# Three of eight experts computed with two products per weight block, a sixth of their blocks unsplit

## The chip, the cores and the metric

The kernel is one program on one core of one Trainium2 chip. The metric is the device time of one execution in microseconds, the median of three runs.

## The reference, cut to what matters

A small network of two blocks runs on 256 tokens of width 1024 in float32. Its last layer, to which the change belongs, is a mixture of eight experts, each a gated feed-forward net of width 3584. A router picks two experts for each token. The reference computes all experts for all tokens and weighs them with the gates, which are zero for experts that a token did not choose:

```
gates = sum of softmax(top 2 logits) * one_hot(top 2 experts, 8)
for e in range(8):
    h_e = silu(t @ w1[e]) * (t @ w3[e])          # 256x1024 @ 1024x3584
    out = out + gates[:, e:e+1] * (h_e @ w2[e])  # 3584x1024
```

## The kernel before

The weights are float32 in the chip's memory and the work runs block by block on them. `Weights` lists all weight keys in order of use; SyncE (SP) loads one 1 MB key at a time into a ring of raw buffers (`load`, L342), and waits for a buffer whose old content has been split. In the expert stage the ring has 15 buffers. Each key is two blocks of 128x1024. `make` splits a block into two float32r halves: ScalarE (ACT) rounds it to `whi` (L371), VectorE (DVE) subtracts to get `wlo` (L372). There are four buffers for each half, and `get` lets `make` run three blocks ahead of the block in use.

[...] Three products stand for one float32 product: high by high, high by low, low by high. A unit is the work on one block; in the expert stage it holds 2 x 3 = 6 products of 512 columns.

The tokens of an expert are gathered into 128 slots (`CAP`). `moe_choose` takes the logits, marks the two largest (`msel`), and counts places with two small products (`mpos`). `moe_slots` makes one-hot matrices `pe`. `moe_gather`, run for two experts at once, multiplies the token halves by `pe` and copies high and low parts of the gathered tokens to `gx`. `moe_units` then orders an expert's units: for each of seven blocks of 512 hidden columns, 4 units of `e1`, 4 units of `e3`, then 4 units of `e2` of the block before. After the last `e1` unit of a block ACT takes a tanh of the sum and DVE multiplies (L2340, L2341); after the last `e3` unit DVE multiplies again (L2345). `turn` transposes the result and splits it into `room` (L429, L430). At the end `moe_scatter` multiplies by the transposed one-hot matrix `ptm` and adds to `acc` (L2504). An expert has 42 keys, so 84 units. The order on PE, ACT and DVE is the order in which the program is written (`manual_schedule`): each engine takes its instructions in that order.

If an expert has more than 128 tokens, a branch at the end (`tc.If(most > over)`) runs the whole stage a second time.

Of the kernel before, what the change touches and what calls it, by code (L numbers as in the profile page):

```python
# [22 lines left out]
P = 128  # L23
# [10 lines left out]
DEEP = 8, 3, 1  # L34
HALVES = slice(0, 64), slice(64, 128)
# [161 lines left out]
def _consts():  # L197
# [34 lines left out]
    c["tie"] = np.zeros((P, 64)) + (np.arange(8)[None, :] < np.arange(8)[:, None]).astype(float).reshape(1, 64)  # L232
    t = np.arange(S)
# [22 lines left out]
LATE = ("flip", "cos", "sin", "rd", "sel", "oh", "ohm", "tri", "ones", "iota", "tie")  # L256
# [51 lines left out]
class Weights:  # L308


    def __init__(self, nc, w, ring, parts, tails, keys, ahead):
        self.nc, self.w, self.ring, self.parts, self.tails = nc, w, ring, parts, tails
        self.subs = []
        off, _ = _offsets()
        for key in keys:
            for i in range(len(off[key][1])):
                self.subs.append((key, i))
        self.ahead = ahead
        self.made, self.used = 0, 0
        self.ready = []  # L320
        self.keys, self.sent, self.loaded = keys, 0, deque()

# [6 lines left out]
    def load(self, between=None):  # L329

        nc = self.nc
        off, subs = _offsets()[0][self.keys[self.sent]]
# [4 lines left out]
        src = self.w[off : off + P * sum(subs)].rearrange("(p n w) -> p n w", p=P, n=n)  # L337
# [12 lines left out]

    def make(self):
# [9 lines left out]
        res = []  # L361
        for tail in range(1 + (subs[i] > 1024)):
# [23 lines left out]
class Net:  # L386
# [1928 lines left out]
    def moe_units(self, st, e, gather, scatter, first, last):  # L2315

        nc = self.nc
        loc = {"h": []}
        p = st["p"]

        def up(nm, nb, kh, i):
            def g(hi, lo):
                if kh == 0 and i == 0:
                    loc[nm] = self.bank("mm")
                xh, xl = st["xh", e], st["xl", e]
                for kk in range(2):
                    k = kh * 4 + i * 2 + kk
                    wh, wl = hi[:, kk * 512 : kk * 512 + 512], lo[:, kk * 512 : kk * 512 + 512]
                    self.mm(loc[nm], xh[:, k, :], wh, k == 0, False)
                    self.mm(loc[nm], xh[:, k, :], wl, False, False)  # L2330
                    self.mm(loc[nm], xl[:, k, :], wh, False, k == 7)
                if kh == 1 and i == 1:
                    act(nm, nb)

            return g

        def act(nm, nb):
            if nm == "e1":
                t = self.keep.tile([P, 512], F32, name="mt", tag="sq_acc")
                nc.scalar.activation(t, loc["e1"], AF.Tanh, scale=st["rs", e][:, 0:1])  # L2340
                nc.vector.scalar_tensor_tensor(t, t, 1.0, loc["e1"], op0=ALU.add, op1=ALU.mult)  # L2341
                loc["t"] = t
            else:
                t = loc["t"]
                nc.vector.scalar_tensor_tensor(t, t, st["rs", e][:, 1:2], loc["e3"], op0=ALU.mult, op1=ALU.mult)  # L2345
                loc["done"] = t

        def turn(a=0, z=4):
            t = loc["done"]
            ps = self.bank()  # L2350
            for i in range(a, z):
                self.transpose(ps[:, i * P : i * P + P], t[:, i * P : i * P + P])
            hh, hl = st["act"]
# [3 lines left out]
        def down(j, i):  # L2357
            def g(hi, lo):
# [62 lines left out]
    def moe_gather(self, st, e):  # L2421
# [7 lines left out]
        def part(c2):  # L2429
            def f():  # L2430
                if c2 == 0:
                    loc["t"] = [self.keep.tile([P, 8, 2, P], F32R, name="gx", tag=tag) for tag in ("xgh", "xgl")]
                    for a in range(2):
                        st["xh", e + a], st["xl", e + a] = [t[:, :, a, :] for t in loc["t"]]
                pe, t = loc["pe"], loc["t"]
                for part, src in enumerate((st["hh"], st["hl"])):
# [6 lines left out]
                    o = t[part][:, 2 * c2 : 2 * c2 + 2].rearrange("p c a s -> p (c a s)")  # L2443
                    if part and e == 0:
                        nc.vector.tensor_copy(o, ps)
                    else:
                        nc.scalar.activation(o, ps, AF.Copy)
# [62 lines left out]
    def moe_slots(self, st, e, n=2):  # L2510

        pe = st["q"].tile([P, 2, 2, P], F32R, name="pe", tag="pe")
        for a in range(n):
            for th in range(2):
                pos, sel = st["pos"][:, th, e + a : e + a + 1], st["sel"][:, th, e + a : e + a + 1]
                self.nc.vector.tensor_scalar(pe[:, th, a, :], st["iota"], pos, sel, op0=ALU.is_equal, op1=ALU.mult)
# [41 lines left out]
    def moe_load(self, st):  # L2558
# [3 lines left out]
        for k in ("tri", "ones", "iota", "tie"):  # L2562
# [38 lines left out]
    def moe_choose(self, st):  # L2601
# [28 lines left out]
        st["sel"] = sel.bitcast(F32).rearrange("p (a e) -> p a e", a=2)  # L2630
# [16 lines left out]
        num = q.tile([P, 8], F32, name="num")  # L2647
        self.copy(num, cnt[:, 0:8])
        st["num"] = num
        st["sq"] = self.squares(self.x, 3, nc.gpsimd)  # L2650

    def moe_prelude(self, st, p):
# [11 lines left out]
        def gates():  # L2664
            st["most"] = q.tile([P, 1], F32, name="most")
            nc.vector.tensor_reduce(st["most"], st["num"], axis=AX.X, op=ALU.max)
            lg, sel = st["lg"], st["sel"]
            mx = q.tile([P, 2], F32, name="lmx")
# [11 lines left out]
        return [scales, gates]  # L2680
# [35 lines left out]
def _program(tc, io, out, tap=None, stop=None, over=CAP):  # L2716
    nc = tc.nc
    with ExitStack() as ctx:
# [27 lines left out]
        with tc.tile_pool(name="moe", bufs=1) as p:  # L2746
            deeper = net.ws.deepen(net.open_pool, DEEP[2])[0]
            st["row"] = (deeper, io["rows"][1:2, :].partition_broadcast(P))
            net.moe_all(st, net.run, net.moe_prelude(st, p), out)
# [3 lines left out]
            most = nc.values_load(flag[0:1, 0:1], min_val=0, max_val=S)  # L2753
            with tc.If(most > over):
                nc.vector.tensor_scalar(st["pos"], st["pos"], -float(CAP), None, op0=ALU.add)
                for f in net.moe_gather(st, 0):
                    f()
                net.ws = Weights(nc, io["w"], deque([net.raw] * 3), net.parts, None, _moe_keys(), 3)
                net.moe_all(st, net.run, [], None)
# [15 lines left out]
```

## Time and profile before

| | us |
|---|---|
| median of 3 runs | 2690.24 (2688.87 to 2690.79) |
| the profiled execution | 2689.64 |
| its span, first to last instruction | 2687.8 |
| PE busy in the span | 2635.4 (98%) |
| DVE busy | 2060.2 (77%) |
| ACT busy | 1607.8 (60%) |

The expert stage is the last thousand microseconds of the span: the first product with gathered tokens (`gx`) starts at 1666.7 us and the last with hidden units (`room`) at 2672.2 us. PE is busy nearly all of the time, and the profile counts pipelined products that overlap only once, so a busy PE says how long its queue was never empty.

### The profile page before, as it was taken

How to read it: one execution, taken by the hardware profiler on the slowest of the kernel's cores; microseconds unless marked ns; L12 is line 12 of the kernel's file. 1: busy time of each engine (PE TensorE's matmuls, PEld its weight loads, DVE VectorE, ACT ScalarE, POOL GpSimd, SP SyncE). 2: the span in 40 equal slices, each digit the busy share in tenths (PEclk: the TensorE clock that was granted, in tenths of full speed). 3: DMA queues.
4: the chain of work that ended last, by engine and by line, in shares of the span. 5: the costliest groups of instructions: out<-in, count | busy, mean ns of one | idle time of the engine just before them, and what ended most of it. 6: DMA issues, size and time to landing. Idle time of an engine off the chain costs nothing.

```text
span 2687.8 us, 44169 instructions
## 1 busy us (share of the span) xinstructions
PE 2635.4 (98%) x17854; PEld 2401.2 (89%) x17854; DVE 2060.2 (77%) x2581; ACT 1607.8 (60%) x2153; POOL 131.3 (5%) x130
## 2 busy tenths in 40 slices
PE   8999999999999999999999999999999999999998
PEld 7989999999989999999999999878887888787876
DVE  5875767556784766557866677999999999999997
ACT  4433555445533555445644456777777777777776
POOL 0032000000012100000000000000000000000000
PEclk9999999999999999999999999999999999999999
DMA  6423534545432543544385445999899989998991
GB/s 245 144 87 108 203 142 165 188 180 202 146 99 92 188 158 126 187 177 157 127 312 187 172 155 206 367 352 366 327 360 354 359 330 358 360 358 330 359 358 59
DMA packets 100285, 614.80 MB, mean 229 GB/s; under 512 B 10664, under 2 KB 20392, under 8 KB 32232
## 3 DMA queue, kind: packets, MB, share of 16 engines
q1 hardware_dynamic: 99352, 609.78, 61.7%
q8 instruction: 142, 2.33, 0.4%
q0 software_dynamic: 720, 2.11, 0.2%
q14 instruction: 71, 0.58, 0.1%
HBM read 609.22 MB, written 2.11 MB: 227 GB/s over the span
## 4 chain that ended last, share of the span: by engine, by line
PE 90%; DVE 5%; issue 3%; ACT 1%; POOL 0%; DMA 0%; SPq 0%; ACTq 0%; DVEq 0%; POOLq 0%
PE ps_mm L422 59%; PE ps_b L422 29%; PE ps_b L426 2%; DVE wlo L372 2%; ACT whi L371 1%; DVE xgl L509 0%; ACT xgh L508 0%; DMA wraw<-in_w 0%; DVE room L430 0%; DVE mt L2341 0%; DVE acc L2504 0%; DVE xc L1894 0%; POOL st_tm_y L451 0%; POOL hn_v L451 0%; POOL tk L1174 0%
## 5 line engine op out<-in xcount | busy, mean ns | idle before, releaser
L372 DVE TENSOR_TENSOR wlo<-wraw,whi 128x1024 fp32r<-128x1024 f32 (+1 forms) x1129 | 1366.2, 1230 | 382.7 <-ACT whi L371 372.6
L371 ACT ACTIVATE whi<-wraw 128x1024 fp32r<-128x1024 f32 (+1 forms) x1129 | 1177.7, 1055 | 754.9 <-PE ps_mm L422 565.0
L422 PE MATMUL ps_mm<-xgh,whi 128*128 128x256 f32 x2048 | 589.0, 288 | 10.8 <-ACT whi L371 7.4
L422 PE MATMUL ps_mm<-whi,gx 128*128 128x512 f32 x1792 | 591.2, 400 | 0.0
L422 PE MATMUL ps_mm<-xgh,wlo 128*128 128x256 f32 x2048 | 582.2, 285 | 4.6 <-DVE wlo L372 4.6
L422 PE MATMUL ps_mm<-xgl,whi 128*128 128x256 f32 x2048 | 582.6, 285 | 0.0
L422 PEld LDWEIGHTS ps_mm<-whi,gx 128*128 128x128 f32 x1792 | 337.5, 188 | 79.3 <-issue 0.5
L422 PEld LDWEIGHTS ps_mm<-xgh,whi 128*128 128x128 f32 x2048 | 391.3, 191 | 15.6 <-ACT whi L371 7.4
L422 PEld LDWEIGHTS ps_mm<-xgh,wlo 128*128 128x128 f32 x2048 | 388.8, 190 | 6.3 <-DVE wlo L372 6.1
L422 PEld LDWEIGHTS ps_mm<-xgl,whi 128*128 128x128 f32 x2048 | 389.4, 190 | 2.3 <-issue 1.4
L422 PE MATMUL ps_mm<-wlo,gx 128*128 128x512 f32 x896 | 355.0, 396 | 0.2 <-DVE wlo L372 0.2
L422 PE MATMUL ps_b<-whi,room 128*128 128x512 f32 x896 | 294.6, 397 | 0.0
L422 PEld LDWEIGHTS ps_mm<-wlo,gx 128*128 128x128 f32 x896 | 168.8, 188 | 39.1 <-issue 0.7
L422 PEld LDWEIGHTS ps_b<-whi,room 128*128 128x128 f32 x896 | 168.3, 188 | 39.4 <-issue 0.2
L422 PE MATMUL ps_b<-hl,whi 128*128 128x256 f32 x688 | 194.5, 283 | 0.0
L422 PE MATMUL ps_b<-hh,wlo 128*128 128x256 f32 x688 | 194.4, 283 | 0.0
L422 PE MATMUL ps_b<-hh,whi 128*128 128x256 f32 x688 | 193.9, 283 | 0.0
L422 PE MATMUL ps_b<-wlo,room 128*128 128x512 f32 x448 | 176.8, 395 | 0.0
L422 PEld LDWEIGHTS ps_b<-hh,wlo 128*128 128x128 f32 x688 | 132.0, 192 | 0.0
L422 PEld LDWEIGHTS ps_b<-hl,whi 128*128 128x128 f32 x688 | 131.9, 192 | 0.0
L422 PEld LDWEIGHTS ps_b<-hh,whi 128*128 128x128 f32 x688 | 131.5, 192 | 0.2
L422 PEld LDWEIGHTS ps_b<-wlo,room 128*128 128x128 f32 x448 | 84.2, 188 | 19.4 <-issue 0.2
(545 smaller groups left out, 3562.6 us busy)
## 6 DMA issues: line engine op xcount, KB each, us to landing
wraw<-in_w SPq DMA_DIRECT2D x557, 1024.0 KB, 5.5
wrawt<-in_w SPq DMA_DIRECT2D x32, 256.0 KB, 4.7
wraw<-in_w SPq DMA_DIRECT2D x8, 512.0 KB, 3.3
cmpw<-in_cmpw SPq DMA_DIRECT2D x2, 1024.0 KB, 7.3
mem<-in_memt SPq DMA_DIRECT2D x2, 1024.0 KB, 7.9
wraw<-in_w SPq DMA_DIRECT2D x2, 560.0 KB, 5.9
x<-in_xt SPq DMA_DIRECT2D x4, 256.0 KB, 5.7
c_rd<-in_cst SPq DMA_DIRECT2D x2, 512.0 KB, 7.6
```

The source lines that it names most:

```text
L371: nc.scalar.activation(hi[:, c], src[:, c], AF.Copy)
L372: nc.vector.tensor_sub(lo[:, c], src[:, c], hi[:, c].bitcast(F32))
L422: self.nc.tensor.matmul(out, lhsT, rhs, start=start, stop=stop, **kw)
L426: self.nc.tensor.transpose(out, in_, self.ident[:k, :k])
```

## The change

The eight experts get places 0 to 7 that are not their numbers any more. Expert 0 keeps place 0. The other seven are ranked by the number of tokens that chose them; the three with the fewest take places 1, 3 and 5 and are called light, and have 64 slots (`LCAP`) instead of 128. The router's tables are reordered by place (`moe_places`, `placed`), and the loads of places 1 to 7 take their address from a register of SP, which is filled from the table `place` (`places`).

A light expert has the 64 slots twice: columns 0 to 63 of the stationary operand hold the high part of the tokens, columns 64 to 127 the low part. One product with `whi` and one with `wlo` then give all four partial products, in two halves of the rows. After each `e1` and `e3` sum, `fold` copies the lower half from PSUM with ACT, and one product by an identity adds it to the upper half; this product is put after the next unit's products (`late`). For `e2` the same doubling is used and the scatter adds the halves.

In a light expert every first block of the keys `e3` with `kh` 0 and of every second `e2` key is not split (`whole`): 14 of 84 blocks. There PE multiplies the raw float32 block in two full float32 products instead of four float32r ones.

If a light expert has more than 64 tokens or another more than 128, the branch at the end runs the second pass.

```diff
+LIGHT, LCAP = (1, 3, 5), 64
...
+    heavy = [p for p in range(N_EXP) if p not in LIGHT]
+    c["rank"] = np.zeros((P, 8)) + np.argsort(np.array(heavy + list(LIGHT)))[None, :]
+    c["lead"] = np.zeros((P, 8)) + 1e6 * (np.arange(8) == 0)[None, :]
...
+        self.place, self.light = {}, ()
+        self.stride = off["e1", 1, 0, 0][0] - off["e1", 0, 0, 0][0]
...
-        off, subs = _offsets()[0][self.keys[self.sent]]
+        key = self.keys[self.sent]
+        off, subs = _offsets()[0][key]
         self.sent += 1
         pool = self.ring.popleft()
         self.ring.append(pool)
         n, m = len(subs), min(subs[0], 1024)
-        src = self.w[off : off + P * sum(subs)].rearrange("(p n w) -> p n w", p=P, n=n)
+        size = P * sum(subs)
+        if key[0] in ("e1", "e2", "e3") and key[1]:
+            src = self.w[bass.ds(self.place[key[1]] * self.stride + (off - key[1] * self.stride), size)]
+        else:
+            src = self.w[off : off + size]
+        src = src.rearrange("(p n w) -> p n w", p=P, n=n)
...
+    def whole(self, key, i):
+
+        if key[0] not in ("e1", "e2", "e3") or key[1] not in self.light or i:
+            return False
+        return key[2] % 2 == 1 if key[0] == "e2" else key[0] == "e3" and key[3] == 0
+
     def make(self):
         nc = self.nc
         key, i = self.subs[self.made]
@@ -358,8 +376,8 @@
             self.cur, self.curt = self.loaded.popleft()
             while len(self.loaded) < len(self.ring) - 4 and self.sent < len(self.keys):
                 self.load()
-        res = []
-        for tail in range(1 + (subs[i] > 1024)):
+        res = [self.cur[i], None] if self.whole(key, i) else []
+        for tail in range(0 if res else 1 + (subs[i] > 1024)):
...
+        loc = {"h": [], "late": None}
         p = st["p"]
+        light = e in st["light"]
+        rows = slice(0, LCAP) if light else slice(0, P)
+
+        def late():
+            f, loc["late"] = loc["late"], None
+            if f:
+                f()
+
+        def fold(nm, nb):
+
+            k = 0 if nm == "e1" else 4
+            b, ps = st["fold", e][LCAP:, k : k + 4, :], loc[nm]
+            nc.scalar.activation(b, ps[LCAP:, :].rearrange("p (c t) -> p c t", c=4), AF.Copy)
+
+            one = st["act"][1][LCAP:, 0, LCAP:]
+            if nb == 0 and nm == "e1":
+                nc.vector.tensor_copy(one, self.ident[LCAP:, LCAP:])
+
+            def f():
+                self.mm(ps[rows, :], one, b, False, True, skip_group_check=True)
+                act(nm, nb)
+
+            loc["late"] = f
 
         def up(nm, nb, kh, i):
             def g(hi, lo):
@@ -2325,32 +2366,44 @@
                 xh, xl = st["xh", e], st["xl", e]
                 for kk in range(2):
                     k = kh * 4 + i * 2 + kk
+                    if lo is None:
+                        self.mm(loc[nm], xh[:, k, :].bitcast(F32), hi[:, kk * 512 : kk * 512 + 512], k == 0, k == 7)
+                        continue
                     wh, wl = hi[:, kk * 512 : kk * 512 + 512], lo[:, kk * 512 : kk * 512 + 512]
                     self.mm(loc[nm], xh[:, k, :], wh, k == 0, False)
-                    self.mm(loc[nm], xh[:, k, :], wl, False, False)
-                    self.mm(loc[nm], xl[:, k, :], wh, False, k == 7)
+                    self.mm(loc[nm], xh[:, k, :], wl, False, light and k == 7)
+                    if not light:
+                        self.mm(loc[nm], xl[:, k, :], wh, False, k == 7)
+                late()
                 if kh == 1 and i == 1:
-                    act(nm, nb)
+                    (fold if light else act)(nm, nb)
...
+            if light:
+                for i in range(a, z):
+                    self.transpose(ps[:, i * LCAP : i * LCAP + LCAP], t[:, i * P : i * P + P])
+                v = ps[:, a * LCAP : z * LCAP].rearrange("p (c t) -> p c t", t=LCAP)
+                self.split(hh[:, a:z, :LCAP], hh[:, a:z, LCAP:], v)
+                loc["h"] += [(hh[:, i, :], None) for i in range(a, z)]
+                return
...
+                    if lo is None:
+                        self.mm(loc["y"][n], h.bitcast(F32), hi[:, n * 512 : n * 512 + 512], a, z)
+                        continue
                     wh, wl = hi[:, n * 512 : n * 512 + 512], lo[:, n * 512 : n * 512 + 512]
                     self.mm(loc["y"][n], h, wh, a, False)
-                    self.mm(loc["y"][n], h, wl, False, False)
-                    self.mm(loc["y"][n], hl, wh, False, z)
+                    self.mm(loc["y"][n], h, wl, False, z and light)
+                    if not light:
+                        self.mm(loc["y"][n], hl, wh, False, z)
+                late()
...
+                    cs = slice(2 * c2, 2 * c2 + 2)
+                    o = t[part][:, cs].rearrange("p c a s -> p c (a s)")
+                    v = ps.rearrange("p (c s) -> p c s", c=2)
+                    copy = nc.vector.tensor_copy if part and e == 0 else self.copy
+                    if e + 1 not in st["light"]:
+                        copy(o, v)
+                    elif part:
+                        copy(o[:, :, :P], v[:, :, :P])
+                        copy(t[0][:, cs, 1, LCAP:], v[:, :, P + LCAP :])
                     else:
-                        nc.scalar.activation(o, ps, AF.Copy)
+                        copy(o[:, :, : P + LCAP], v[:, :, : P + LCAP])
...
+                if e + a in st["light"]:
+                    out = out.rearrange("p (d s) -> p d s", d=2)
+                    iota = iota[:, :LCAP].unsqueeze(1).to_broadcast([P, 2, LCAP])
+                self.nc.vector.tensor_scalar(out, iota, pos, sel, op0=ALU.is_equal, op1=ALU.mult)
...
+        cnt = self.bank()
+        for th in range(2):
+            self.mm(cnt[:, 0:8], st["onesr"], sel[:, 8 * th : 8 * th + 8], th == 0, th == 1)
         self.moe_turn(st, 3, "hh", self.copy)
+        one = self.moe_places(st, cnt, gt, ge, tie)
+
+        def placed(out, src):
+            t = ge.rearrange("p a b c -> p a b c")
+            nc.vector.tensor_tensor(t, src.unsqueeze(2).to_broadcast([P, 2, 8, 8]), one.unsqueeze(1).to_broadcast([P, 2, 8, 8]), op=ALU.mult)
+            nc.vector.tensor_reduce(out, t, axis=AX.X, op=ALU.add)
+
+        placed(num, chosen)
+        nc.vector.tensor_copy(sel, num.rearrange("p a e -> p (a e)"))
         base(0, 1)
...
+        placed(num, lg)
+        nc.vector.tensor_copy(lg, num)
+        pl = num[:, 0, :]
+        nc.vector.tensor_tensor(ge[:, 0], one, st["iota"][:, 0:8].unsqueeze(1).to_broadcast([P, 8, 8]), op=ALU.mult)
+        nc.vector.tensor_reduce(pl, ge[:, 0], axis=AX.X, op=ALU.add)
+        place = st["place"] = q.tile([P, 8], I32, name="place")
+        nc.vector.tensor_copy(place, pl)
...
+        n = t.tile([P, 2, 8], F32, name="load")
+        nc.vector.tensor_tensor(n[:, 0, :], cnt[:, 0:8], st["lead"], op=ALU.add)
+        a0 = n[:, 0:1, :].to_broadcast([P, 8, 8])
+        a1 = n[:, 0, :].unsqueeze(2).to_broadcast([P, 8, 8])
+        g, h = gt[:, 0], ge[:, 0]
+        nc.vector.tensor_tensor(g, a0, a1, op=ALU.is_gt)
+        nc.vector.tensor_tensor(h, a0, a1, op=ALU.is_ge)
+        nc.vector.copy_predicated(g, tie[:, 0], h)
+        nc.vector.tensor_reduce(n[:, 1, :], g, axis=AX.X, op=ALU.add)
+        one = gt[:, 1]
+        rank = st["rank"].unsqueeze(2).to_broadcast([P, 8, 8])
+        nc.vector.tensor_tensor(one, n[:, 1:2, :].to_broadcast([P, 8, 8]), rank, op=ALU.is_equal)
+        return one
...
+        def places():
+            for e in range(1, N_EXP):
+                self.ws.place[e] = nc.values_load(
+                    st["place"][0:1, e : e + 1], engines=(mybir.EngineType.SP,), min_val=0, max_val=N_EXP - 1
+                )
+
+        return [scales, lambda: (gates(), places())]
```

## Rows read from the trace of the kernel before

**Rows 1.** Busy time, and DMA in 40 slices of the span (page).

```profile
PE 2635.4 (98%) x17854; PEld 2401.2 (89%) x17854; DVE 2060.2 (77%) x2581; ACT 1607.8 (60%) x2153; POOL 131.3 (5%) x130
...
DMA  6423534545432543544385445999899989998991
```

**Rows 2.** Two experts: busy us (instructions) of PE, PEld, DVE, ACT, POOL; clock, DMA share, GB/s.

```profile
1930.00:2180.00 250.00, 248.96 (x1118) 201.29 (x1117) 232.40 (x233) 196.40 (x212) 0.00 (x0) 1.00 0.93 351
```

**Rows 3.** Groups of instructions in the same stretch: busy us, mean ns, idle before.

```profile
L372 DVE TENSOR_TENSOR wlo<-wraw,whi 128x1024 fp32r<-128x1024 f32 x168 | 200.3, 1221 | 15.9 <-ACT whi L371 14.0
L371 ACT ACTIVATE whi<-wraw 128x1024 fp32r<-128x1024 f32 x168 | 175.5, 1059 | 37.1 <-PE ps_mm L422 22.8 <-PE ps_b L422 14.0
...
L430 DVE TENSOR_TENSOR room<-ps_b,room 128x512 fp32r<-128x512 f32 (+1 forms) x20 | 12.7, 634 | 1.7 <-ACT room L429 1.1
L429 ACT ACTIVATE room<-ps_b 128x512 fp32r<-128x512 f32 (+1 forms) x20 | 11.1, 554 | 11.6 <-PE ps_b L426 11.6
L2345 DVE SCALAR_TENSOR_TENSOR mt<-mt,rs,ps_mm 128x512 f32<-128x512 f32 x14 | 10.4, 741 | 0.0
...
L2504 DVE SCALAR_TENSOR_TENSOR acc<-ps_b,gate,acc 128x512 f32<-128x512 f32 x7 | 5.2, 743 | 0.0
```

**Rows 4.** Waits in the expert stage, 1680 to 2620 us: total us, times, longest us.

```profile
ACT whi L371 <- PE ps_mm L422: 83.8, 217, 1.6
ACT whi L371 <- PE ps_b L422: 53.5, 160, 0.3
DVE wlo L372 <- ACT whi L371: 49.3, 184, 1.1
```

**Rows 5.** Timeline of two units on ACT, with DVE: start, length, instruction, [idle before].

```profile
1836.38 1.06 ACT L371 ACTIVATE whi<-wraw 128x1024 fp32r<-128x1024 f32 x1 [0.34 <-PE ps_b L422]
...
1837.47 1.22 DVE L372 TENSOR_TENSOR wlo<-wraw,whi 128x1024 fp32r<-128x1024 f32 x1 [0.17 <-ACT whi L371]
...
1837.78 1.06 ACT L371 ACTIVATE whi<-wraw 128x1024 fp32r<-128x1024 f32 x1 [0.34 <-PE ps_b L422]
```

**Rows 6.** Timeline of PE around one full float32 product, shown as two records.

```profile
2625.02 1.02 PE L422 MATMUL ps_mm<-acc,t_ident 128*128 128x512 f32 x2
2625.48 0.79 PE L422 MATMUL ps_b<-whi,room 128*128 128x512 f32 x1
2626.11 0.39 PE L422 MATMUL ps_b<-wlo,room 128*128 128x512 f32 x1
```

**Rows 7.** Timeline of the routing, DVE and PE.

```profile
1660.00 0.29 DVE L2628 TENSOR_REDUCE num<-gt 128x16 f32<-128x128 f32 x1
1660.32 0.17 DVE L2631 TENSOR_SCALAR msel<-num 128x16 fp32r<-128x16 f32 x1
...
1661.19 0.17 DVE L2642 COPY mpos<-ps_b 128x16 f32<-128x16 f32 x1
1661.40 1.11 DVE L2516 TENSOR_SCALAR pe<-c_iota,mpos,msel 128x128 fp32r<-128x128 f32 x4
...
1662.40 0.79 PE L422 MATMUL ps_b<-pe,hh 128*128 128x256 f32 x4 [0.43 <-DVE pe L2516]
```

**Rows 8.** Three stretches, columns as in group 2.

```profile
1350.00:1360.00 10.00, 10.00 (x86) 10.00 (x85) 4.24 (x8) 4.13 (x6) 0.18 (x1) 1.00 0.98 391
1680.00:1720.00 40.00, 40.00 (x180) 32.19 (x178) 37.99 (x37) 31.36 (x33) 0.00 (x0) 1.00 0.98 376
2000.00:2100.00 100.00, 99.48 (x441) 79.99 (x440) 94.19 (x95) 77.77 (x85) 0.00 (x0) 1.00 0.95 358
```

**Rows 9.** SP: its waits at 2000 to 2100 us; loads from 1640 us; issues.

```profile
SPq L342 <- DVE wlo L372: 87.1, 34, 3.4
...
wraw<-in_w SPq DMA_DIRECT2D x326, 1024.0 KB, 6.6
wraw<-in_w SPq DMA_DIRECT2D x2, 512.0 KB, 7.0
...
L342 SPq DMA_DIRECT2D wraw<-in_w x567: 327/328/943, 1.7 to 2622.4; - x189
```

More of the change, by code (lines that the diff above doesn't have):

```diff
@@ L2338, in act @@
             if nm == "e1":
-                t = self.keep.tile([P, 512], F32, name="mt", tag="sq_acc")
-                nc.scalar.activation(t, loc["e1"], AF.Tanh, scale=st["rs", e][:, 0:1])
-                nc.vector.scalar_tensor_tensor(t, t, 1.0, loc["e1"], op0=ALU.add, op1=ALU.mult)
+                t = self.keep.tile([P, 512], F32, name="mt", tag="sq_acc")[rows, :]
+                nc.scalar.activation(t, loc["e1"][rows, :], AF.Tanh, scale=st["rs", e][rows, 0:1])
+                nc.vector.scalar_tensor_tensor(t, t, 1.0, loc["e1"][rows, :], op0=ALU.add, op1=ALU.mult)
                 loc["t"] = t
@@ L2434, in f @@
                         st["xh", e + a], st["xl", e + a] = [t[:, :, a, :] for t in loc["t"]]
+                    if e + 1 in st["light"]:
+                        st["fold", e + 1] = st["xl", e + 1]
                 pe, t = loc["pe"], loc["t"]
@@ L2561, in moe_load @@
         nc.sync.dma_start(rt, self.io["router"].rearrange("p (c e) -> p c e", c=8))
-        for k in ("tri", "ones", "iota", "tie"):
+        for k in ("tri", "ones", "iota", "tie", "rank", "lead"):
             st[k] = self.load_const(q if k == "iota" else st["t"], k)
@@ L2664, in gates @@
         def gates():
-            st["most"] = q.tile([P, 1], F32, name="most")
+            few = q.tile([P, 3], F32, name="few")
+            st["most"] = few[:, 2:3]
+            for e in LIGHT:
+                nc.vector.tensor_scalar(st["num"][:, e : e + 1], st["num"][:, e : e + 1], float(CAP - LCAP), None, op0=ALU.add)
             nc.vector.tensor_reduce(st["most"], st["num"], axis=AX.X, op=ALU.max)
             lg, sel = st["lg"], st["sel"]
-            mx = q.tile([P, 2], F32, name="lmx")
+            mx = few[:, 0:2]
             gate = st["gate"] = q.tile([P, 2, N_EXP], F32, name="gate")
@@ L2748, in _program @@
             st["row"] = (deeper, io["rows"][1:2, :].partition_broadcast(P))
+            st["light"] = net.ws.light = LIGHT
             net.moe_all(st, net.run, net.moe_prelude(st, p), out)
@@ L2752, in _program @@
             nc.vector.tensor_copy(flag, st["most"][0:1, :])
-            most = nc.values_load(flag[0:1, 0:1], min_val=0, max_val=S)
+            most = nc.values_load(flag[0:1, 0:1], min_val=0, max_val=2 * S)
             with tc.If(most > over):
-                nc.vector.tensor_scalar(st["pos"], st["pos"], -float(CAP), None, op0=ALU.add)
+                st["light"], places = (), net.ws.place
+                for e in range(N_EXP):
+                    cap = LCAP if e in LIGHT else CAP
+                    nc.vector.tensor_scalar(st["pos"][:, :, e], st["pos"][:, :, e], -float(cap), None, op0=ALU.add)
                 for f in net.moe_gather(st, 0):
```

24 lines of the change are left out of this document (11 added, 13 removed).

## The prediction

> **What bounds the kernel now.** I read the page first: PE is busy 98% of the span, and in the last 15 of 40 slices, the expert stage, the DMA share is 8 or 9 tenths too but for the very last [rows 1]. So two things have to be asked there: what PE's work would be, and whether the weights can come faster. The windows give the stage its measure. Two experts, one even and one odd, take 250.0 us: they hold 168 `wlo` [rows 3], which is 2 x 84 units. [...] Third, SP: of 100 us it waits 87.1 for a raw buffer to come free [rows 9]. The weights are ahead of the work, and 358 GB/s [rows 8] is what the work asks for, not what the memory can give.
>
> **The price of a unit.** ACT starts a `whi` every 1.40 us, each released by PE [rows 5]: six products, 0.233 us each. 84 units are 117.6 us of an expert's 125.0; transposes, scatter and gather are the rest. A full float32 product is in the trace too, the identity by `acc`: from its start at 2625.02 to the start of the second product after it at 2626.11 are 1.09 us [rows 6], less one product of 0.233: 0.857 us. [...]
>
> **PE in a light expert.** A split unit falls from six to four products, 0.933 us. A whole unit is two full products, 1.714 us. So 70 x 0.933 + 14 x 1.714 = 65.3 + 24.0 = 89.3 us, and 14 folds of 0.233 add 3.3: 92.6 against 117.6, 25.0 saved. The odd experts also hold the gather for the next two, so they take some 127 us now (an estimate from the 250.0: 32 products of half width, 3.7 us, sit in the odd one only). PE then needs 102 us.
>
> **DVE and ACT in a light expert.** DVE: 232.4 / 2 = 116.2, less 14 x 1.19 (200.3 / 168) = 16.7 for the blocks that aren't split, less about 2 for the narrower split after `turn` (12.7 us for 20 [rows 3]): 97.5 us. ACT: 196.4 / 2 = 98.2, less 14 x 1.045 = 14.6, plus 14 copies of 128x512 at 0.55 (11.1 for 20 on L429 [rows 3]) = 7.7, plus 2 for the gather's copies, which go out in three pieces instead of two: 93 us. PE is still the longest, but DVE's slack is 4.5 us in 102.
>
> **What this near-balance costs.** The work is not level within an expert. The first eight units have no `e2` among them: PE has 7 x 0.933 + 1.714, a fold and eight scatter products, 10.4 us; DVE has 7 x 1.19 + 2 x 0.74 + 2 x 0.63 + 4 x 0.743 [rows 3] = 14.0. PE waits some 3.5 us there. In the later blocks of twelve units PE has 13.7 us and DVE 13.8, so what PE loses there isn't won back. A split buffer's way round is 0.34 to wake ACT, 1.06 `whi`, 0.17, 1.22 `wlo` [rows 5], 2.8 us, and three further split units on PE take 2.8 us: level again. Into this loop comes the fold: ACT's copy waits for the product to end, and behind it in ACT's order stand the next `whi`, and through it DVE's next `wlo`. After `e1` the next unit is a whole one, long and without a buffer, which covers the copy; after `e3` it is a split one, and I count 0.55 us for each of six: 3.3. Together 7 us, so 109 us for a light expert and 18 saved. Bounds: nothing, if the three blocks of lookahead take up all of it (102 us, 25 saved); and a full chain for each of 14 folds, 0.34 + 1.06 + 0.55 + 0.1 less the unit beside it of 0.933, 1.1 us each, 15 us (117 us, 10 saved). Three experts: 54, from 30 to 75.
>
> **The routing.** Nothing but small work runs on PE between the choice `msel` and the first gather, so the new steps are on the path. Before the places are counted: a product and nine small DVE steps; then six more ahead of `pe`, because DVE takes them in order. Steps of this kind start 0.32 us apart and a round over PE takes 0.87 (1660.32 to 1661.19) [rows 7]. Of the 15 steps half are narrower; at 0.25 to 0.32 they are 3.8 to 4.8, and part of the round is hidden by the transposes that PE still has: 5 us, bounds 2 and 7. The four more copies in the first gather lie beside PE's products.
>
> **Loads by register.** 294 of 336 loads take their address from a register. SP spends 0.33 us on an issue [rows 9] and waits 87 of 100 us, so up to 2.8 us more on each costs nothing. No row shows such a load. Its bounds are nothing and, once uncovered, what goes beyond 2.8 us; I take nothing, as it is nearest to the plain issue. The seven register reads stand in SP's queue with the loads of expert 0 behind them; at an issue's largest 0.94 us they are 7 us, and some twelve landed blocks, 35 us of work, cover them. Without that cover PE would wait these 7 us once.
>
> **Does the stream keep up?** A light expert in 109 us asks for 42 x 1.0486 MB / 109 = 404 GB/s, a heavy one 352. The ring evens this out. By the forecast the sixth expert ends at about 1667 + 5 + 3 x 232 = 2368 us and needs 252 loads, two more being split ahead. From 1640 us there are 327 keys [rows 9], so nine came earlier, and 245 must land in 728 us: 2.97 us each, 353 GB/s. The trace has 376 over 40 us and 391 over 10 us [rows 8]. So the stream holds, without much to spare.
>
> **Sum.** 2689.64 - 54 + 5 = 2640.6 for the profiled execution; the median of the runs lies 0.6 higher: 2641. Bounds: 2689.6 - 75 + 2 = 2616 and 2689.6 - 30 + 7 = 2667.
>
> **Rivals.**
> First, the stream paces the light experts. For it: DMA shares of 0.95 and more at 358 [rows 8]; against it the 376 and 391. If only 345 GB/s came, 245 loads would take 745 us, 17 more: 2658. [...]
> Second, the folds stall in full: 117 us a light expert, 2667.
> Third, PE alone counts and nothing waits: 2619.
> Fourth, slower than before: the register-addressed loads hold SP. From the last product with `room` to the end are 15.6 us; with 7 to land and 2.4 to split, the end can't come before 1640 + 327 loads + 25. That passes 2689.6 from 3.13 us a load; at 4 us for each of the 294 it would be 1640 + 33 x 2.94 + 294 x 4 + 25 = 2938. For it: nothing is known of the path. Against it: the issue is 0.33 now.
> Fifth, the change doesn't do what it says: a light expert has over 64 tokens, the second pass runs, and the time is some 1000 us more. The reference's router on its default inputs gives the three lightest of experts 1 to 7 24, 38 and 41 tokens, and no expert over 104.
>
> **Chances.** The forecast 0.66; stream 0.13; folds in full 0.06; PE alone 0.05; register loads 0.05; second pass 0.02; gains that cancel against waits that I don't see 0.03. A measurement of this kernel can tell 0.2%, 5.4 us. The cases faster than that hold 0.90, none 0.03, slower 0.07. From 2616 to 2666 the first four cases lie almost whole, with the forecast's own spread of lumps and routing in it: about 0.8.
>
> **What would show it.** Light experts of about 109 us between heavy ones of 123 to 127; in them 70 `wlo` each and 28 full products in pairs of records; PE's idle in them some 7 us, released by DVE `wlo` and, at folds, by ACT; DVE above 90% busy. The first `gx` product at about 1672. DMA over 390 GB/s in light experts, with SP waiting for buffers less than before. Wrong would be: PE waiting for `wraw` to land, SP busy without waits, light experts above 117 us, or a span with a second pass.

## The result, and the profile after

The changed kernel takes 2655.65 us (median of 4 runs, 2654.52 to 2656.97) against 2689.65 for the kernel before (4 runs): a ratio of 0.9873, 95% interval 0.9856 to 0.9891. It is faster by 34 us, where 49 were forecast. The profiled execution took 2656.97 us, its span 2655.2.

The page of the changed kernel, busy times and DMA in 40 slices, against [rows 1]:

```profile
PE 2589.7 (98%) x17394; PEld 2310.9 (87%) x17394; DVE 2010.9 (76%) x2564; ACT 1575.5 (59%) x2161; POOL 131.9 (5%) x130
...
DMA  7332544554432443454466444799999999999991
```

PE (TensorE) is still the busiest engine by far, and DMA has gone up by up to a digit in the expert stage. The page can't say where the 34 us come from; marks in the trace can. I use three: DVE's copy of the logits `lg`, the first product with `gx`, and the DVE step `rs`, which comes once per pair of experts.

The `rs` marks of the changed kernel (timeline of DVE; start, length):

```profile
1681.28 0.16 DVE L2524 TENSOR_SCALAR rs<-ps_b 128x2 f32<-128x2 f32 x1
...
1914.32 0.15 DVE L2524 TENSOR_SCALAR rs<-ps_b 128x2 f32<-128x2 f32 x1
...
2151.13 0.15 DVE L2524 TENSOR_SCALAR rs<-ps_b 128x2 f32<-128x2 f32 x1
...
2389.61 0.15 DVE L2524 TENSOR_SCALAR rs<-ps_b 128x2 f32<-128x2 f32 x1
```

And in the kernel before:

```profile
1670.64 0.16 DVE L2458 TENSOR_SCALAR rs<-ps_b 128x2 f32<-128x2 f32 x1
...
1918.14 0.15 DVE L2458 TENSOR_SCALAR rs<-ps_b 128x2 f32<-128x2 f32 x1
...
2170.05 0.15 DVE L2458 TENSOR_SCALAR rs<-ps_b 128x2 f32<-128x2 f32 x1
...
2421.96 0.15 DVE L2458 TENSOR_SCALAR rs<-ps_b 128x2 f32<-128x2 f32 x1
```

The differences, in us:

| stretch | before | after | change |
|---|---|---|---|
| start to `lg` | 1658.92 | 1663.04 | +4.1 |
| `lg` to first `gx` product (routing) | 7.77 | 14.30 | +6.5 |
| first pair of experts | 247.50 | 233.04 | -14.5 |
| second pair | 251.91 | 236.81 | -15.1 |
| third pair | 251.91 | 238.48 | -13.4 |
| last `rs` to the end | 265.8 | 265.6 | -0.2 |

Each pair holds one light expert, so a light expert gives 13.4 to 15.1 us, where 18 were forecast; the three give 43.0. The routing takes 6.5 where 5 were forecast. The last 4.1 lie ahead of the routing, in a part that the change leaves nearly as it was. There `lg` comes anywhere from 1654.9 to 1666.1 us in the eleven traces of this study that share the new routing, also between two executions of the same changed kernel (1663.04 and 1664.24).

Most of this spread is PE's clock. These are 50 us ahead of the routing, in the kernel before, in the changed kernel and in the kernel with the earliest `lg`, the one with the slots in another place (columns as in [rows 2]):

```profile
765.00:815.00 50.00, 46.10 (x343) 42.06 (x342) 41.28 (x76) 19.96 (x39) 15.91 (x16) 0.90 0.25 79
...
765.00:815.00 50.00, 45.00 (x319) 40.41 (x318) 43.19 (x77) 19.28 (x37) 14.89 (x15) 0.86 0.25 84
...
765.00:815.00 50.00, 46.88 (x358) 42.18 (x357) 42.15 (x78) 21.14 (x41) 15.96 (x16) 0.93 0.24 80
```

An estimate, from the profile read in stretches of 8.7 us (the length of each, times what its clock lacks to 1.00): ahead of `lg` 25.7 us are lost to the clock before and 29.0 after, so 3.3 of the 4.1; over the eleven traces it is 20.6 to 29.1. What is left of the time to `lg` is 1633 to 1637 us in all of them and in the kernel before. Why the clock is lower in one execution than in another stays open. So a median carries some us that belong to no edit, and below I read edits of a few us from the stretches.

The pairs have such falls too, and by the same estimate one costs 1.7 us: none before, one in the changed kernel, in the third pair. Without it that pair would save 15.1, as the second does.

**A light expert.** Windows of the changed kernel (length, busy us of PE, PEld, DVE, ACT, POOL, clock, DMA share, GB/s): one whole light expert, then pieces of it:

```profile
1800.00:1913.00 113.00, 109.56 (x429) 71.23 (x427) 99.03 (x105) 89.55 (x115) 0.00 (x0) 1.00 0.98 393
1800.00:1825.00 25.00, 23.05 (x87) 14.82 (x86) 22.72 (x25) 18.68 (x24) 0.00 (x0) 1.00 0.93 341
1825.00:1850.00 25.00, 25.00 (x93) 15.82 (x93) 22.96 (x23) 20.57 (x25) 0.00 (x0) 1.00 1.00 405
1875.00:1900.00 25.00, 24.08 (x89) 14.82 (x87) 23.20 (x29) 20.90 (x25) 0.00 (x0) 1.00 1.02 422
```

Its groups of instructions in the same 113 us (busy us, mean ns of one, idle before):

```profile
L390 DVE TENSOR_TENSOR wlo<-wraw,whi 128x1024 fp32r<-128x1024 f32 x70 | 83.1, 1219 | 10.8 <-ACT whi L389 10.8
...
L440 PE MATMUL ps_mm<-gx,room 64*64 64x512 f32 x14 | 6.2, 441 | 0.0
```

There are the 70 `wlo`, the 14 folds, and idle of PE of 113.0 - 109.6 = 3.4 us: the forecast had 7. Waiting isn't what cost the 18 us. In the middle of the expert, 1825 to 1850, PE never idles at all, and yet a block of twelve units takes 14.50 us, where 13.7 were forecast: the turns of three blocks in a row stand at 1815.95, 1830.44 and 1844.95. Something on PE is longer than I had it. The timeline of PE and of its weight loads (PEld) around one fold shows it:

```profile
1832.80 1.88 PE L440 MATMUL ps_mm<-wraw,gx 128*128 128x512 f32 x4
...
1834.61 0.13 PEld L440 LDWEIGHTS ps_mm<-gx,room 64*64 64x64 f32 x1 [0.76 <-ACT gx L2350]
1834.61 0.45 PE L440 MATMUL ps_mm<-gx,room 64*64 64x512 f32 x1
...
1834.98 0.19 PEld L440 LDWEIGHTS ps_mm<-whi,gx 128*128 128x128 f32 x1 [0.25 <-issue]
1834.98 0.50 PE L440 MATMUL ps_mm<-whi,gx 128*128 128x512 f32 x1
1835.09 0.19 PEld L440 LDWEIGHTS ps_mm<-wlo,gx 128*128 128x128 f32 x1
...
1835.32 0.40 PE L440 MATMUL ps_mm<-wlo,gx 128*128 128x512 f32 x1
```

From 1832.80 to 1835.32 there are two full float32 products (1.71), the fold and one product (0.233): the fold's share is 0.57 us, not 0.233. The weight loads show where it goes. Between the products of 128 by 128 around it a load starts 0.23 us ahead of its product (1835.09 for 1835.32), beside the product before it. The fold's load and that of the product behind it start only with their products, at 1834.61 and 1834.98: nothing overlaps there. The releaser that the row names, ACT's copy, is not the reason: that copy ran from 1833.24 to 1833.83, 0.78 us ahead. The fold is the one product on 64 rows and 64 columns among products of 128 by 128. No run tells what in that form costs the time. By the rows it is 0.57 - 0.233 = 0.34 us a fold, and 14 x 0.34 are 4.8 us per light expert.

**The routing.** The timeline of the changed kernel, against [rows 7]:

```profile
1664.44 0.17 DVE L2701 TENSOR_SCALAR msel<-num 128x16 fp32r<-128x16 f32 x1
...
1664.76 0.42 PE L440 MATMUL ps_b<-msel,onesr 128*128 128x8 f32 x2 [1.75 <-DVE msel L2701]
...
1669.51 2.06 DVE L2586 TENSOR_SCALAR pe<-c_iota,mpos,msel 128x128 fp32r<-128x128 f32 x4
1670.17 1.31 POOL L515 TENSOR_TENSOR sq_acc<-sq_acc,sq_t 128x512 f32<-128x512 f32 x1 [9.97 <-ACT sq_t L514]
...
1671.62 1.01 PE L440 MATMUL ps_b<-pe,hh 128*128 128x256 f32 x3 [0.56 <-DVE pe L2586]
```

From `msel` to the first `pe` are 5.07 us against 1.08 [rows 7]: 4.0 more, inside the 3.8 to 4.8 that I counted. Behind it two things came that I hadn't counted. The four `pe` take 2.06 us against 1.11, while the addition `sq_acc` runs beside them on POOL (GpSimd, another engine). And the gather's products take 0.21 us each (1672.43 to 1673.28 for four) instead of 0.12 (1663.02 to 1663.49 before): PE had idled, 1.75 us at the longest, and the granted clock is 0.80 over these 25 us, where it was 1.00 before:

```profile
1650.00:1675.00 25.00, 21.17 (x152) 20.01 (x152) 16.97 (x40) 10.67 (x20) 3.98 (x4) 0.80 0.65 241
```

### The profile page after: what moved, and what is told of

Same layout as the page of the kernel before. It is cut to its first block, busy times and chain, and to the rows that moved or that the text cites. A ratio compares the mean times of both kernels' runs of the same rounds, so it can differ in the third digit from the quotient of the medians.

```text
span 2655.2 us, 43918 instructions
## 1 busy us (share of the span) xinstructions
PE 2589.7 (98%) x17394; PEld 2310.9 (87%) x17394; DVE 2010.9 (76%) x2564; ACT 1575.5 (59%) x2161; POOL 131.9 (5%) x130
## 4 chain that ended last, share of the span: by engine, by line
PE 86%; DVE 7%; issue 3%; ACT 2%; POOL 1%; DMA 1%; SPq 0%; DVEq 0%; POOLq 0%; ACTq 0%
PE ps_mm L440 56%; PE ps_b L440 28%; DVE wlo L390 3%; PE ps_b L444 2%; ACT whi L389 1%; DVE acc L2570 0%; DMA mem<-in_memt 0%; DVE room L448 0%; DVE mt L2387 0%; DMA wraw<-in_w 0%; ACT xgh L526 0%; DVE xgl L527 0%; DVE pe L2586 0%; DVE xc L1912 0%; POOL st_tm_y L469 0%
## 5 line engine op out<-in xcount | busy, mean ns | idle before, releaser
L390 DVE TENSOR_TENSOR wlo<-wraw,whi 128x1024 fp32r<-128x1024 f32 (+1 forms) x1087 | 1317.7, 1233 | 389.6 <-ACT whi L389 381.5
L389 ACT ACTIVATE whi<-wraw 128x1024 fp32r<-128x1024 f32 (+1 forms) x1087 | 1126.0, 1053 | 706.3 <-PE ps_mm L440 530.9
L440 PE MATMUL ps_mm<-whi,gx 128*128 128x512 f32 x1414 | 491.1, 402 | 0.0
L440 PE MATMUL ps_mm<-wlo,gx 128*128 128x512 f32 x854 | 338.2, 396 | 0.5 <-DVE wlo L390 0.5
L440 PEld LDWEIGHTS ps_mm<-whi,gx 128*128 128x128 f32 x1414 | 266.2, 188 | 67.4 <-issue 6.3
L440 PE MATMUL ps_b<-whi,room 128*128 128x512 f32 x686 | 243.2, 411 | 0.0
L440 PEld LDWEIGHTS ps_mm<-wlo,gx 128*128 128x128 f32 x854 | 160.9, 188 | 37.5 <-DVE wlo L390 1.0
L440 PEld LDWEIGHTS ps_b<-whi,room 128*128 128x128 f32 x686 | 129.2, 188 | 36.8 <-issue 8.6
L440 PE MATMUL ps_b<-wlo,room 128*128 128x512 f32 x406 | 160.5, 395 | 0.0
L440 PEld LDWEIGHTS ps_b<-wlo,room 128*128 128x128 f32 x406 | 76.5, 188 | 23.1 <-issue 4.8
```

The costliest lines, as they stand in the source:

```text
L389: nc.scalar.activation(hi[:, c], src[:, c], AF.Copy)
L390: nc.vector.tensor_sub(lo[:, c], src[:, c], hi[:, c].bitcast(F32))
L440: self.nc.tensor.matmul(out, lhsT, rhs, start=start, stop=stop, **kw)
```

## Experiments

The kernels were timed beside the kernel before, whose medians there were 2689.66, 2689.85 and 2692.43 us. The changed kernel run again gave 2656.55 us, ratio 0.987 [0.9855, 0.9886], and the same three pairs within 0.1 us:

> The changed kernel once more, as the measure for the three beside it: 2653 to 2657. Between executions its time should go with the mean granted clock, as it does in the runs so far.

**One fold on all rows.** If the form of 64 by 64 is what costs, a fold on 128 rows and 128 columns should be cheap. The identity gets a zero half, and ACT copies both halves:

```diff
-            b, ps = st["fold", e][LCAP:, k : k + 4, :], loc[nm]
-            nc.scalar.activation(b, ps[LCAP:, :].rearrange("p (c t) -> p c t", c=4), AF.Copy)
+            b, ps = st["fold", e][:, k : k + 4, :], loc[nm]
+            nc.scalar.activation(b, ps.rearrange("p (c t) -> p c t", c=4), AF.Copy)
...
-                self.mm(ps[rows, :], one, b, False, True, skip_group_check=True)
+                self.mm(ps, one, b, False, True, skip_group_check=True)
```

> The fold's copy takes all 128 rows and its product uses a stationary matrix of 128x128 instead of 64x64; place in the order and result stay the same. Theory (the smaller tile): a fold costs PE 0.57 us instead of 0.23 because it is the only product here on a 64x64 part of the array; with the full one a block of twelve units falls from 14.5 to about 13.8 us, a light expert from 113 to 108, and the time from 2655.7 to about 2641 (2639 to 2646). Rival (the copy): the fold waits for ACT's copy of the sum; then nothing changes, 2653 to 2658.

Measured: 2647.57 us, ratio 0.984 [0.9827, 0.9854]. PE in this kernel, around a fold in the `e2` units:

```profile
1828.08 0.40 PE L440 MATMUL ps_b<-whi,room 128*128 128x512 f32 x1
1828.43 0.50 PE L440 MATMUL ps_b<-wlo,room 128*128 128x512 f32 x1
1828.77 0.40 PE L440 MATMUL ps_b<-whi,room 128*128 128x512 f32 x1
1829.00 0.40 PE L440 MATMUL ps_b<-wlo,room 128*128 128x512 f32 x1
1829.23 0.40 PE L440 MATMUL ps_mm<-gx,room 128*128 128x512 f32 x1
1829.47 0.39 PE L440 MATMUL ps_b<-whi,room 128*128 128x512 f32 x1
```

The fold now takes 0.24 us, like any product, in the same place and with a larger copy ahead of it. So the form was the cost, not the copy that I had feared. But the pairs shrink by 0.9, 2.5 and 2.5 us only, not by 4.8. The second line shows why: the product with `wlo` starts 0.35 after the one before it instead of 0.233, as `wlo` isn't ready (its weight load waits 0.40 us for DVE). Over the three pairs (waits, 1680 to 2420 us) the weight loads' waits for `wlo` grow from 3.3 to 6.9 us, and PE's waits for `mt` and `room` from 11.6 to 15.0, the largest being

```profile
PE ps_b L444 <- DVE mt L2392: 10.1, 6, 1.8
```

Of the 3 x 4.8 = 14.4 us, 5.9 come out and some 7 turn into waits for DVE and ACT. Another 1.7 go to a fall of the clock in the first pair, behind an idle of 1.56 us; the changed kernel idled 1.35 at that turn, and its clock held:

```profile
1819.42 0.46 PE L444 MATMUL ps_b<-t_ident,mt 64*128 64x64 f32 x4 [1.56 <-DVE mt L2392]
...
1814.00:1824.00 10.00, 8.44 (x31) 6.16 (x30) 8.15 (x9) 5.36 (x7) 0.00 (x0) 0.83 0.94 343
```

The median is 8 us lower than the changed kernel's; how much of that lies ahead of the routing isn't known, as the profiled execution was the slowest of the five (2654.74). The next bound is DVE, 7% behind PE before the change [rows 2] and, as the prediction counted it, 4.5 us behind in a light expert's 102.

**No light experts.** All eight experts get 128 slots and six products; the ranking, the reordered tables and the loads by register stay:

```diff
-LIGHT, LCAP = (1, 3, 5), 64
+LIGHT, LCAP = (), 64
```

> No light experts: all eight have 128 slots and three products; ranking, tables by place, register reads and loads by register stay. Theory: the routing costs 6.5 us and the loads nothing: 2689.7 + 6.5 = 2696 (2694 to 2699), and two experts still take 250 to 252 us. Rival: the register loads or something ahead of the routing cost too (the changed kernel's routing began 4 us late in its profile): 2700 or more.

Measured: 2696.58 us, ratio 1.0028 [1.0018, 1.0038]. The pairs take 247.60, 252.03 and 252.01, as before to 0.1 us, with 294 loads by register in the stage. So these loads cost nothing that shows. The routing (`lg` to the first `gx` product) takes 15.50 here, 7.7 more than before; the total grows by 6.9 only, as the stretch behind the last `rs` is 1.2 shorter in this trace.

**No unsplit blocks.** Every block is split; a light expert has 84 units of four products:

```diff
-        if key[0] not in ("e1", "e2", "e3") or key[1] not in self.light or i:
+        if key[0] not in ("e1", "e2", "e3") or key[1] not in self.light or True:
```

> No block is left unsplit; the light experts split all 84 blocks and have two products for each. Theory: PE's work falls to 97 us a light expert, but DVE's rises to 115, which then bounds, with 3 to 5 us of waits on top: 118 to 120 instead of 113, the time 2671 to 2677. Rival: the unsplit blocks are not worth it, as their full products cost PE what DVE saves: 2650 to 2660.

Measured: 2671.84 us, ratio 0.9937 [0.9922, 0.9952]. The pairs save 8.8, 9.5 and 9.3 us instead of 14.5, 15.1 and 13.4. The window and the longest DVE group:

```profile
1800.00:1913.00 113.00, 99.98 (x391) 65.13 (x390) 109.43 (x117) 97.28 (x117) 0.00 (x0) 0.98 0.97 385
```

```profile
L390 DVE TENSOR_TENSOR wlo<-wraw,whi 128x1024 fp32r<-128x1024 f32 x82 | 95.6, 1211 | 1.5 <-ACT whi L389 1.4
```

PE idles 13 of 113 us and DVE is busy 97% of them. With four products a unit and every block split, the split is the bound; giving a sixth of the blocks to PE whole, at 1.71 us instead of 0.93, is worth some 16 us by the medians. In the pairs it is 15.4, of which about 3.4 are the clock: it falls once in each of the three here, once in all in the changed kernel.

**Slots and gate product in other places.** In the changed kernel PE waits for `mt` at the first and last block of a light expert, 8.5 us in all up to 2420 us, and never in the kernel before:

```profile
PE ps_b L444 <- DVE mt L2391: 8.5, 6, 1.5
```

In the last block DVE makes the `pe` slots of the next gather ahead of the `mt` that PE is waiting for. This kernel puts the slots three units later, and in a light expert's first full block the turn after four units instead of two:

```diff
-        if slots:
-            units.append(("x", slots))
-        units += between(downs(5), [lambda: turn(0, 2), lambda: turn(2, 4)], 2)
+        last6 = between(downs(5), [lambda: turn(0, 2), lambda: turn(2, 4)], 2)
+        if slots:
+            last6.insert(3 if light else 0, ("x", slots))
+        units += last6
...
-between(product("e1", nb), [turn] if nb else first or scatter, 2)
+between(product("e1", nb), [turn] if nb else first or scatter, 4 if light and nb == 1 else 2)
```

> In light experts the one-hot matrices for the next gather are made after the first transposes of the last block instead of ahead of its e2 units, and the transposes of the first block come after four units of e1 instead of two. Theory: PE's two waits for DVE's last product there, 1.35 and 1.49 us in the first light expert, go, and with them, in the execution where it happened, a fall of the clock: 2 to 3 us a light expert, 2646 to 2650. Rival: DVE is behind in these stretches anyway and the wait only moves: 2653 to 2657.

Measured: 2644.86 us, ratio 0.9835 [0.9822, 0.9849]. The pairs take 231.44, 235.09 and 235.20: 1.6, 1.7 and 3.3 less, 6.6 in all; the same wait falls to 3.7 us. The median is 11 us lower; in the profiled execution (2642.41) 8.2 us lie ahead of the routing, where no edit is and the estimate gives 8.4 us less lost to the clock. The third pair wins more because there, in the changed kernel, the clock fell behind the idle of 1.50 us: its four records of full float32 products at 2374.42 take 3.36 us, where those behind the same turn in the first light expert, at 1900.83, take 1.98, and the granted clock is below 1:

```profile
2375.00:2400.00 25.00, 24.41 (x112) 18.44 (x111) 17.14 (x22) 17.73 (x24) 0.00 (x0) 0.93 0.87 332
```

In this kernel it is 1.00 there.

**The order of the routing.** For the clock in the routing I first tried to keep PE's small work for the time in which it waits. With PE's pause of 1.75 us gone and the clock held at 1.00, the 2.5 us by which the first gather is longer (7.83 us from `pe` to the first `gx` product, 5.29 before) should come back, for 2652 to 2654 us. The second half of the transposes goes ahead of the count:

```diff
+        self.moe_turn(st, 3, "hh", self.copy)
+        base(0, 1)
+        base(1, 1)
         cnt = self.bank()
...
-        self.moe_turn(st, 3, "hh", self.copy)
         one = self.moe_places(st, cnt, gt, ge, tie)
...
-        base(0, 1)
-        base(1, 1)
```

> In the routing the transposes of the tokens (four of the high part and eight for the sums) are put ahead of the product that counts the experts' tokens, so that PE has work while DVE finds the two largest logits. [...] Rival: the chain on DVE sets the time anyway and the clock falls all the same: 2655 to 2657.

Measured: 2652.39 us, ratio 0.9861 [0.9846, 0.9877]. The median is 3 us lower, but not through this: the clock is 0.80 as before, and `lg` to the first `gx` product takes 14.85 us, 0.55 more. The gain lies ahead of `lg` (1657.19 against 1663.04). The theory fell: the same work in another place leaves as much idle; a wait of 2.29 us now follows where 1.75 stood before. The pairs, in which nothing was edited, take 234.79, 238.23 and 236.82 here: 1.8 and 1.4 longer and 1.7 shorter, as the clock falls once in each of the first two and not in the third. So a difference of that size in a pair is read as an edit's only where the clock held in both traces.

**Products that compute nothing.** So 15 products whose result nobody reads fill PE's idle in the routing, 7 after the choice, 2 after the places, 6 before `pe`. With the clock held at 1.00, the gather's products should take 0.12 us again instead of 0.21, and the choice to the first `gx` product 10.5 us instead of 12.9, for 2652 to 2654 us:

```diff
+        def filler(n):
+            ps = self.bank("mm")
+            for i in range(n):
+                self.mm(ps, hi[:, 0, 0:P], hi[:, 0:2, :].rearrange("p a t -> p (a t)"), True, True)
+
+        filler(7)
...
+        filler(2)
...
+        filler(6)
```

> Fifteen products of 512 columns that nothing reads are put into the routing where PE would wait: seven ahead of the count, two beside the ranking, six ahead of the gather. They add work and change no result. [...] Rival: the steps on DVE set the time and the fillers stand in the way: 2655 or more.

Measured: 2657.39 us, ratio 0.9872 [0.9857, 0.9888]: no difference in the total. In the trace the clock holds, also in the routing itself, which comes late here (1.00 from 1666 to 1680 us):

```profile
1650.00:1675.00 25.00, 22.68 (x178) 20.32 (x176) 19.73 (x42) 12.20 (x22) 4.52 (x4) 1.00 0.63 238
```

and the gather's products take 0.12 instead of 0.21 us, but `lg` to the first `gx` product falls by 1.0 us only, to 13.28. The four `pe` take 2.65 us here, and PE waits for them.

**The squares earlier.** In all traces with the new routing so far, one of the four `pe` takes 1.29 to 1.33 us instead of 0.34, always while POOL's `sq_acc` runs; before the change `sq_acc` began after them (1663.08). This kernel moves the last squares from the end of `moe_choose` to its start:

```diff
+        st["sq"] = self.squares(self.x, 3, nc.gpsimd)
         lg = st["lg"] = q.tile([P, 2, N_EXP], F32, name="lg")
...
-        st["sq"] = self.squares(self.x, 3, nc.gpsimd)
```

> Only the place of the last squares changes: ACT's sq_t and POOL's two sq_acc additions move from the end of the choice to its start, before the copy of the logits. In every run of the changed kernel so far one of the first four pe steps on DVE took 1.29 us instead of 0.34, while POOL's 1.31 us sq_acc ran; in the kernel before, sq_acc began after the four. Theory (DVE and POOL hold each other up): the four pe steps take 0.34 each, and from the choice to the first product with gx it is about 1 us less than 12.9. Rival (another cause of the long step, such as PE's lower clock): one pe step still takes 1.29. Second rival: the hold-up only moves, and one of the small DVE steps behind the logits grows by about 1 us; the stretch from the copy of the logits to that product is then as long as before. The total moves by less than 2 us, too little to tell.

Measured, in one execution: 2655.81 us. DVE and POOL:

```profile
1664.28 1.32 POOL L515 TENSOR_TENSOR sq_acc<-sq_acc,sq_t 128x512 f32<-128x512 f32 x1 [3.66 <-ACT sq_t L514]
...
1664.53 0.29 DVE L2699 TENSOR_REDUCE num<-gt 128x16 f32<-128x128 f32 x1
1664.85 0.78 DVE L2702 TENSOR_SCALAR msel<-num 128x16 fp32r<-128x16 f32 x1
...
1670.66 1.11 DVE L2586 TENSOR_SCALAR pe<-c_iota,mpos,msel 128x128 fp32r<-128x128 f32 x4
```

The four `pe` are back at 1.11 us, so POOL was the cause; the rival with the clock is out, for the clock is still 0.80 here. But `msel`, the step that now falls under `sq_acc`, takes 0.78 instead of 0.17: more than half of the gain moves there, and `lg` to the first `gx` product is 13.81, 0.5 less. The reduction beside the same `sq_acc` is as long as ever (0.29).

**The edits together.** Fold on all rows, the turn's transposes on all 128 rows too, the other places for slots and turn, and the filler products; then the same with the squares moved.

> Four edits together: the fold on the full array, the light experts' tanh and products on all 128 rows so that their transposes too use the full array, the later one-hot matrices and transposes, and the fillers. Theory: 8 from the fold as measured, some 3 from the transposes (0.16 us for each of 21), 7 from the waits, 2.5 from the clock, less what DVE, then the longest, keeps: 2634 to 2642. Rival: DVE bounds the light experts once the fold is cheap, and the rest gives nothing: 2645 to 2648.

Measured: 2633.08 us (2631.03 to 2635.12), ratio 0.9784 [0.9771, 0.9798], 1 us below the range expected.

> The four earlier edits (fold on all rows with full transposes, slots and gate product in other places, filler products in the routing) plus the moved squares. Theory: with the clock kept up and no hold-up on pe, the choice to the first gx product takes 10 us or less instead of 11.9 in the run of the four; the rest as there, so about 2631 us against 2633. Rival: another step sets the gather, and the stretch stays at 11.9.

Measured: 2635.07 us (2631.07 to 2635.45), ratio 0.978 [0.9766, 0.9793]; between the two there is no difference to be told. In the traces the pairs take 227.2, 230.8 and 230.9 us in both, and `lg` to the first `gx` product 13.28 and 12.37. In the last one `pe` to the first `gx` product takes 5.34 us, against 5.29 before the change and 7.83 after: the clock and POOL account for all of it, and what is left of the routing's cost are the new DVE steps and 0.6 us by which `msel` is held up. From the choice (`msel`) to the first `gx` product it is 10.97 us, where 10 or less were expected, against 11.88 without the moved squares. No pair of these two traces has a fall of the clock. A whole light expert and the start of the next one, in the first of the two kernels:

```profile
1790.00:1920.00 130.00, 127.04 (x526) 91.29 (x525) 120.36 (x133) 104.23 (x133) 0.00 (x0) 1.00 1.00 403
```

Both beat the kernel before by 2.2%, and by their medians the changed kernel by 0.8 to 0.9%.

## Why the prediction was right, and where it was off

The sign, the cause and the range held; the predicted gain of 49 us was 15 too large. By its own steps:

- **What bounds.** Right. PE set the pace, DVE was next. The 232.4 and 196.4 us that the prediction halves for an expert are DVE's and ACT's busy times in [rows 2]; ACT waited for PE and DVE for ACT [rows 4]. The order showed in both directions: without the unsplit blocks DVE bounds (97% busy), and with cheap folds PE waits for `wlo`.
- **Four products a unit, two full ones for a whole unit.** Right: two full products take 1.72 us from 1829.11 on in the kernel with all edits, counted to the product behind the fold less one product, against 1.714. The price read from [rows 6] held.
- **Fold at 0.233.** The step that failed, and the largest. It measured 0.57, because of its form of 64 by 64: 14 x 0.34 = 4.8 us a light expert. I had looked for the cost of a fold in ACT's copy and the chain behind it, counted at 3.3 us, and took the product itself for one like the rest. The trace before has no product on fewer than 128 rows in this stage, and I gave it no bound of its own. Earlier stages of it have some, and show a part of the price: products of 128 rows and 256 columns start every 0.12 us there, the first one of 64 rows comes 0.21 after the last of them, and its load starts only with it.

```profile
1314.84 0.28 PE L422 MATMUL ps_mm<-wlo,xgh 128*128 128x256 f32 x1
1314.95 0.28 PE L422 MATMUL ps_mm<-whi,xgl 128*128 128x256 f32 x1
1315.16 1.13 PE L422 MATMUL ps_b<-k,q 64*128 64x256 f32 x8
...
1315.16 0.73 PEld L422 LDWEIGHTS ps_b<-k,q 64*128 64x128 f32 x8
```

- **Transposes.** Taken as unchanged. On 64 rows a turn and the product after it take 1.06 us from the last product (1844.62 to 1845.68), on 128 rows, in the kernel with all edits, 0.90 to 0.92: 0.14 to 0.16 x 7, some 1.0 us.
- **Waits of 7 us.** They were 3.4 by PE's idle. The first block, counted at 3.5, has 1.8 (idles of 0.48 and 1.35); the chain behind `e3` folds did not show. Instead there was one of 1.49 in the last block, from the slots, that I had not seen. So 25.0 - 4.8 - 1.0 - 3.4 = 15.8 us should be saved, and the second pair saves 15.1. DVE was busy 99.0 of 113 us, near the 97.5 that I had counted, but 88% and not above 90%. That the waits came out small is no independent stroke of luck: the dear folds gave DVE the time. In the kernel with cheap folds the second light expert idles 4.5 us on PE and waits another 2.3 with weight loads for `wlo`, 6.8 together, and the second pair, in which the clock never falls, saves 17.6 of the 18. The largest of these waits (2033 to 2151 us):

```profile
PE ps_b L444 <- DVE mt L2392: 3.4, 2, 1.8
...
PEld ps_b L440 <- DVE wlo L390: 2.3, 6, 0.4
```

- **Routing +5.** It was 6.5. The DVE steps were 4.0, as counted. The rest are two effects of the longer path: behind PE's idle the clock was 0.80 (1.00 with the 15 products put into it), and POOL's squares came to lie beside `pe` (2.06 us for the four instead of 1.11). The bound of 7 held here, not in the kernel without light experts, where it was 7.7 in the trace.
- **Register loads at nothing.** Right, by the kernel that has them and no light experts.
- **The stream.** Right. DMA ran at 393 GB/s over a light expert and at 405 to 422 in its later parts, above the 391 that the trace before showed, and PE never waited for `wraw`; SP still waited for free buffers for most of the stage (1680 to 2620 us), less than the 812.8 us before:

```profile
SPq L354 <- DVE wlo L390: 649.0, 301, 5.8
```

- **The sum.** Of the 16.4 us by which the spans' difference of 32.6 falls short of 49, the pairs are 11.0 (54 - 43.0), the routing 1.5, and 4.1 lie ahead of `lg`, less 0.2 at the end. Of the 11.0, 1.7 are the fall of the clock in the third pair; of the 4.1, 3.3 are the clock too, by the estimate above. The forecast had no term for either. What makes the clock fall there in one execution and not in another stays open.

## What to carry to other kernels

Where products are in a long row of equal shape, price one of another shape by itself, even if its columns are the same: here 64 by 64 among products of 128 by 128 was dearer (0.57 us) than a product padded to 128 by 128 with zeros (0.24). An earlier stage with a mix of shapes may show part of that price before anything is built. When the bound engine's work is cut by a fifth and the next engine is 7% behind, look for work that can be moved to the bound engine at a good price, as the unsplit blocks do. And when a stretch of small steps gets longer, look at what comes to lie beside it, and at PE's clock behind the idle (0.80 in the routing here, 1.00 with 15 products put into it).

## What the runs showed that I had not expected

- One 64 by 64 product among 128 by 128 ones cost 0.57 us, where one of 128 by 128 cost 0.23 to 0.24.
- An idle of 1.5 to 1.8 us of PE was followed by longer products in the routing (0.21 us instead of 0.12) and in the third pair (3.36 instead of 1.98 for two full products), while idles of 1.35 and 1.49 us in the first light expert had no such effect (clock 1.00). Products without use kept the clock at 1.00 in the routing.
- The clock's falls differ between executions of kernels that share the code: about 21 to 29 us are lost to them ahead of the routing, by the estimate above, and 1.7 us in a pair of experts that has a fall.
- A DVE `pe` step of 0.34 us became 1.29 us under one POOL addition of 1.31 us, and `msel` went from 0.17 to 0.78, while a reduction beside the same addition kept its 0.29.
- Loads from memory reached 422 GB/s over 25 us on this one core.
